# A seventh accumulator in the opening of an fp32 layer, its sums and transposes in one PSUM bank, and the modulation rows in runs of eight

## The chip, the cores and the metric

The kernel runs on one core of a Trainium2 chip. The metric is the device time of one execution, in microseconds (us). The shape is one sequence of 512 tokens with a model width of 1024, all in fp32.

## The reference

One layer: a feed-forward block, a mixer of mLSTM and attention with a forget gate, and a second feed-forward block. Each norm is modulated by rows that come from a small vector `c` by one product with `w_ada` (1024 x 9216).

```python
mod = jax.nn.silu(c) @ w_ada + b_ada
sh1, sc1, g1, sh2, sc2, g2, sh3, sc3, g3 = [m[:, None, :] for m in jnp.split(mod, N_MOD, axis=-1)]
u = rms_norm(x, ffn1_norm_g) * (1 + sc1) + sh1
x = x + 0.5 * g1 * swiglu(u, ffn1_w_in, ffn1_w_out)
...
def swiglu(u, w_in, w_out):
    a, b = jnp.split(u @ w_in, 2, axis=-1)
    return (jax.nn.silu(a) * b) @ w_out
```

The change lies in the first feed-forward block's `u @ w_in` (1024 x 5632: 22 column blocks of 128 for `a` and 22 for `b`) and in the rows of `mod` that are computed beside it.

## The kernel before, in words

Every fp32 product is made of three products of reduced-precision parts: `uh` and `ul` are the high part and the rest of the activations, `wh` and `wl` those of the weights. ACT makes a high part (L117), DVE the rest (L119). `mm3` (L142 to L144) issues hi x hi, hi x lo and lo x hi. In a slot 24 matmuls of 512 columns run behind one weight tile of 128 x 1024 (512 KB).

**The opening** is `start` (from L940). It loads `x`, computes the norm, and has 8 slices k of 128 of the model width. For each slice there are columns of `w_ada` (`ar`, four DMAs of 256 KB: shift v = 0 and scale v = 1, two halves each) and weights `raw` (block columns 0 to 2 of `a` and of `b`). Slice 0's shift and scale are summed over the 1024 rows by PE alone (`mod0`, 16 matmuls of 128 columns), slice 1's in part by PE (`mod1`) and otherwise by DVE; for slices 2 to 7, DVE makes products `ac` (`mod`, L1003) and PE adds up the partitions (`sums`, L1018). ACT turns the two sums into `m` (L1020, L1021), then `uh` and `uf` from the transposed x (L1026, L1028), and DVE `ul` (L1030). The transposes are `turn` (L977). A slice's gemm (L1084) is three passes over six accumulators, 3 blocks of `a` and 3 of `b`: `uh` with `wh`, `uh` with `wl`, `ul` with `wh`. The transposes of the next slice stand at the 7th matmul, its sums at the 12th. PE, ACT and DVE keep program order here (`pin`). All loads are issued by SP in program order; the weights use three buffers (`raw`), `wh` and `wl` four each.

**The slots** follow: `ffn_in` takes the other 19 blocks, first block 3 alone (two slots, one for `a` and one for `b`, `w_stat`), then 36 slots for pairs. Each calls `slot()`: `tick` runs what is due, `pw` brings one step of preparing the second weight matrix (loads `sa`, `sb`; stores `ws`), and `ada` one step of a modulation row (`ada_row`: 512 KB of `w_ada` in a `raw` buffer, one product on DVE, L323 or L325; eight steps make one row). The rows come in the order v = 3, 4, 2, 6; a slot with n % 6 = 5 has none. Behind the eighth step, `ada_sum` puts six steps into the coming ticks: 1 `fold` (ACT, L364, into a buffer of `wh`), 2 `high` (DVE L368, then ACT L369 into a buffer of `wl`), 3 `low` (DVE, L372), 4 `total` (PE, L377), 6 `bias`, 7 `put`.

PSUM has eight banks here: four from `gbank`, four from `tbank`. The accumulators take four and two, the column sums one (`cb`), the transposes one.

Of the kernel before, what the change touches and what calls it, by code (L numbers as in the profile page):

```python
# [47 lines left out]
class Layer:  # L48
# [261 lines left out]
    def ada_row(self, v, new, new_row, bank):  # L310
# [6 lines left out]
        for k in range(NK):  # L317
# [8 lines left out]
            if k == NK - 1:  # L326
                self.ada_sum(v, parts, new_row, bank)
# [26 lines left out]
    def ada_sum(self, v, parts, new_row, bank):  # L354
# [27 lines left out]
        for n, f in ((1, fold), (2, high), (3, low), (4, total), (6, bias), (7, put)):  # L382
            self.later(n, f)
# [24 lines left out]
    def ffn_in(self, w_in, j0, hp, tp, slot):  # L408

        if j0 % 2:  # L410
            ps = []
            for o in (0, FF):
                wt = self.w_stat(w_in, o + j0 * P)
                slot()
                ps.append(self.gbank())
                self.gemm_stat(ps[-1], wt, 0, T)
            self.pair_h(self.pair_s(ps[0], 0, T, tp), ps[1], j0, 0, T, hp, tp)
            self.lo_after = None
            j0 += 1
# [520 lines left out]
    def start(self, st, tp):  # L940
# [28 lines left out]
        def fill(n):  # L969

            for i in range(n):
                pin(nc.tensor.transpose(cb[:, 384:512], self.ident, self.ident))
# [5 lines left out]
        def ada_load(k):  # L978

            ars[k] = st.tile([P, NK, 2, P], F32, name=self.nm("ar"), tag="ar", bufs=7)  # L980
            halves = [(v, i) for v in range(2) for i in (0, 4)] if k == 0 else [(v, i) for i in (0, 4) for v in range(2)]
            for v, i in halves:
                nc.sync.dma_start(ars[k][:, i:i + 4, v, :], w_ada[i * P:(i + 4) * P, v * D + k * P:v * D + (k + 1) * P]
                                  .rearrange("(i p) n -> p i n", p=P))
        def mod0(v):

            for i in range(NK):
                pin(nc.tensor.matmul(cb[:, 128 * (v + 1):128 * (v + 2)], ars[0][:, i, v, :], self.ccol[:, i:i + 1].to_broadcast([P, P]),
# [15 lines left out]
        sh = [P, 2, NJ0 * P]  # L1004
        def load(k):
            raws[k] = self.raw(sh, [(lambda t, i=i: t[:, i, :],
                                     w_in[k * P:(k + 1) * P, i * FF:i * FF + NJ0 * P]) for i in range(2)])
# [5 lines left out]
        def w_lo(k):  # L1013
            hi, lo = ws[k]
            pin(nc.vector.tensor_tensor(lo, raws.pop(k), hi, op=SUB))
        def sums(k):
            for v in range(2):
                pin(nc.tensor.matmul(cb[:, 2 * k + v:2 * k + v + 1], accs[k][:, v, :], self.one, start=True, stop=True))  # L1018
        def affine(k, m, c, b):
            pin(nc.scalar.activation(m[:, 0:1], c[0], AF.Identity, bias=b[0]))  # L1020
            pin(nc.scalar.activation(m[:, 1:2], c[1], AF.Identity, scale=self.colC[:, 8 + k:9 + k], bias=b[1]))  # L1021
        def u_hi(k):
            m = sp.tile([P, 2], F32, name=self.nm("m"), tag="m", bufs=4)
            c = (cb[:, 2 * k:2 * k + 1], cb[:, 2 * k + 1:2 * k + 2]) if k else (cb[:, 128:129], cb[:, 256:257])
            affine(k, m, c, base if k == 1 else (self.colC[:, 16 + k:17 + k], self.colC[:, 24 + k:25 + k]))
# [5 lines left out]
        for k in range(3):  # L1031
# [6 lines left out]
        acc_ps = [self.gbank() for _ in range(4)] + [self.tbank() for _ in range(2)]  # L1038
        cb = self.tbank()
        fill(30)  # L1040
# [11 lines left out]
        mod0(0)  # L1052
        turn(0, (0, 1))
        turn(1, (0, 1))
        mod0(1)
        turn(0, (2, 3))
        mod1()
        w_hi(0)
        w_lo(0)
        u_hi(0)  # L1060
        mc, mb = [sp.tile([P, 2], F32, name=self.nm("m"), tag="m", bufs=4) for _ in range(2)]
# [10 lines left out]
        for k in range(NK):  # L1072
# [5 lines left out]
            for i, (p, b) in enumerate((p, b) for p in range(3) for b in range(2 * NJ0)):  # L1078
                if n < NK and i == 7:
# [834 lines left out]
```

## Time and profile before

| | us |
|---|---|
| median of 3 runs | 1303.6 |
| lowest, highest | 1303.08, 1305.67 |
| profiled execution | 1304.69 |
| its span | 1302.9 |
| PE busy in the span | 1288.7 (99%) |
| DVE, ACT busy | 982.1 (75%), 657.1 (50%) |

The profile is of one execution. Its span is the time from the first to the last recorded instruction. PE is TensorE's matmuls, PEld its weight loads, DVE VectorE, ACT ScalarE, SP SyncE, which issues most of the DMAs. The page gives PE's granted clock as 9 tenths or more in all 40 slices. A timeline row is one instruction or several of one kind in succession: its start, its length, and in brackets the idle time of the engine before it with what ended that. The length of a matmul (0.39 us for 512 columns) overlaps that of the next, so the step from start to start is what it costs.

### The profile page before, as it was taken

To read this page: it belongs to the slowest core of one execution; us is meant where nothing else is said; L and a number is where in the kernel's file an instruction comes from. 1 tells how busy PE (TensorE), PEld (TensorE's weight loads), DVE (VectorE), ACT (ScalarE), POOL (GpSimd) and SP (SyncE) were. 2 spreads that over 40 slices of the span, in tenths; PEclk is the share of its full clock that TensorE was granted. 3 is DMA by queue.
4 is the path that set the end of the run, shared out by engine and by line. 5 is a ranking of instruction groups with operands and counts; after the bars stand their busy time and mean duration, and the time that the engine had idled before them with its cause. 6 is when DMAs were issued, how large, how long until landed. Compare 5 with 4: busy or idle time off the path is not lost.

```text
span 1302.9 us, 17823 instructions
## 1 busy us (share of the span) xinstructions
PE 1288.7 (99%) x6241; PEld 1080.2 (83%) x6241; DVE 982.1 (75%) x1764; ACT 657.1 (50%) x1086; POOL 34.9 (3%) x73
## 2 busy tenths in 40 slices
PE   7999999999999999999999999999999999999998
PEld 6787888878889888888888888888898888888887
DVE  6877777778788868989897866778977656635787
ACT  5523223256567656666575786343683223223741
POOL 1000000000010011000000100000000000000000
PEclk9999999999999999999999999999999999999999
DMA  9988988765864634556455985776649867634574
GB/s 287 276 287 291 313 291 308 240 177 184 310 184 118 193 108 136 153 151 161 131 127 159 269 184 153 231 245 203 194 136 333 278 228 265 229 99 136 170 264 149
DMA packets 248330, 272.02 MB, mean 209 GB/s; under 512 B 57824, under 2 KB 185472, under 8 KB 248240
## 3 DMA queue, kind: packets, MB, share of 16 engines
q1 hardware_dynamic: 241104, 254.55, 63.3%
q10 hardware_dynamic: 4384, 7.88, 2.0%
q0 software_dynamic: 2752, 8.45, 1.9%
q8 instruction: 49, 0.80, 0.3%
q14 instruction: 41, 0.34, 0.1%
HBM read 227.77 MB, written 43.06 MB: 208 GB/s over the span
## 4 chain that ended last, share of the span: by engine, by line
PE 71%; DVE 4%; ACT 2%; issue 1%; DMA 1%; DVEq 0%; ACTq 0%; SPq 0%
PE g L144 18%; PE g L143 18%; PE g L142 18%; PE t L142 4%; PE t L143 4%; PE t L144 4%; PE t L1500 1%; PE t L1470 1%; PE t L1440 1%; PE t L1441 1%; ACT wh L117 0%; DVE wl L760 0%; DVE wl L119 0%; PE t L299 0%; DVE x L614 0%
## 5 line engine op out<-in xcount | busy, mean ns | idle before, releaser
L117 ACT ACTIVATE wh<-raw 128x1024 fp32r<-128x1024 f32 (+2 forms) x238 | 240.1, 1015 | 355.4 <-DMA raw<-in_ffn_w_in_dram 127.5
L119 DVE TENSOR_TENSOR wl<-raw,wh 128x1024 fp32r<-128x1024 f32 (+2 forms) x238 | 276.6, 1167 | 146.7 <-ACT wh L117 139.5
L144 PE MATMUL g<-uh,wl 128*128 128x512 f32 (+1 forms) x880 | 340.3, 387 | 1.6 <-DVE wl L119 1.6
L142 PE MATMUL g<-uh,wh 128*128 128x512 f32 (+1 forms) x880 | 341.0, 387 | 0.2 <-ACT wh L117 0.2
L143 PE MATMUL g<-ul,wh 128*128 128x512 f32 (+1 forms) x880 | 339.2, 385 | 0.0
L144 PEld LDWEIGHTS g<-uh,wl 128*128 128x128 f32 x880 | 165.3, 188 | 36.6 <-DVE wl L119 3.5
L142 PEld LDWEIGHTS g<-uh,wh 128*128 128x128 f32 x880 | 165.4, 188 | 33.3 <-issue 0.8
L143 PEld LDWEIGHTS g<-ul,wh 128*128 128x128 f32 x880 | 165.4, 188 | 32.6
L142 PE MATMUL g<-wh,uh 128*128 128x512 f32 (+1 forms) x256 | 97.6, 381 | 0.0
L144 PE MATMUL g<-wh,ul 128*128 128x512 f32 (+1 forms) x256 | 96.6, 377 | 0.0
L143 PE MATMUL g<-wl,uh 128*128 128x512 f32 (+1 forms) x256 | 96.5, 377 | 0.0
L325 DVE SCALAR_TENSOR_TENSOR acc<-raw,ccol,acc 128x1024 f32<-128x1024 f32 (+1 forms) x49 | 54.8, 1129 | 46.5 <-DMA raw<-in_w_ada_dram 46.3
L143 PE MATMUL t<-wl,A 128*128 128x512 f32 x176 | 68.6, 390 | 0.8 <-DVE wl L119 0.8
L142 PE MATMUL t<-wh,A 128*128 128x512 f32 x176 | 68.7, 390 | 0.0
L144 PEld LDWEIGHTS g<-wh,ul 128*128 128x128 f32 x256 | 48.2, 188 | 8.9
L143 PEld LDWEIGHTS g<-wl,uh 128*128 128x128 f32 x256 | 48.3, 188 | 8.4
L142 PEld LDWEIGHTS g<-wh,uh 128*128 128x128 f32 x256 | 48.2, 188 | 8.2
L142 PE MATMUL g<-yh,wh 128*128 128x512 f32 x128 | 49.9, 390 | 0.0
L144 PE MATMUL g<-yh,wl 128*128 128x512 f32 x128 | 49.8, 389 | 0.0
L143 PE MATMUL g<-yl,wh 128*128 128x512 f32 x128 | 49.8, 389 | 0.0
L1451 ACT ACTIVATE S<-S,mn 128x128 f32<-128x128 f32 (+1 forms) x64 | 35.6, 557 | 25.2 <-DVE mn L1443 15.8
L465 ACT ACTIVATE A<-E 128x768 fp32r<-128x768 f32 x22 | 18.6, 845 | 51.4 <-DVE E L464 51.0
(403 smaller groups left out, 2295.0 us busy)
## 6 DMA issues: line engine op xcount, KB each, us to landing
raw<-in_ffn_w_in_dram SPq DMA_DIRECT2D x80, 512.0 KB
raw<-in_w_ada_dram SPq DMA_DIRECT2D x48, 512.0 KB
raw<-in_w_mix_dram SPq DMA_DIRECT2D x46, 512.0 KB
sa<-in_ffn_w_out_dram SPq DMA_DIRECT2D x22, 512.0 KB
sb<-in_ffn_w_out_dram SPq DMA_DIRECT2D x44, 256.0 KB
ws<-sa SPq DMA_DIRECT2D x22, 512.0 KB
ws<-sb SPq DMA_DIRECT2D x44, 256.0 KB
raw<-ws SPq DMA_DIRECT2D x44, 256.0 KB
```

Source lines behind the costliest of these rows:

```text
L117: nc.scalar.activation(hi, src, AF.Copy)
L119: self.last_lo = nc.vector.tensor_tensor(lo, src, hi, op=SUB)
L142: pin(mm(ps, lh, rh, start=start, stop=False, skip_group_check=on))
L143: pin(mm(ps, lh, rl, start=False, stop=False, skip_group_check=on))
L144: self.last_mm = pin(mm(ps, ll, rh, start=False, stop=stop, skip_group_check=on))
L325: nc.vector.scalar_tensor_tensor(a, r[:, s], c, a, op0=MUL, op1=ADD)
L465: nc.scalar.activation(A1[:, 0:3, :], E[:, 0:3, :], AF.Copy)
L1440: nc.tensor.matmul(ps[:, :w], q[:, s], k[:, :w], start=True, stop=False)
L1441: nc.tensor.matmul(ps[:, :w], q[:, s], kl[:, :w], start=False, stop=True)
L1451: nc.scalar.activation(S[:, ws], S[:, ws], AF.Exp, scale=-1.0, bias=m, accum_out=sm[:, qb:qb + 1])
L1470: tr = lambda b, c, qb, kb: nc.tensor.transpose(b[:, c:c + P], S[:, P_OFF[qb] + kb * P:P_OFF[qb] + (kb + 1) * P], self.ident)
L1500: nc.tensor.matmul(po[:, q0:], vt[:, kb, i, :], Px[:, o:o + T - q0], start=n == 1, stop=n == 8)
```

## The change

1. The opening has seven accumulators: block 3 of `a` is the seventh. Its weights per slice are 448 KB in place of 384. `ffn_in` starts with block 3 of `b` alone, so there are 37 slots in place of 38; `s3` is the silu of the seventh accumulator.
2. `sums` takes its own `tbank`. Seven accumulators leave one bank to sums and transposes together, which now take turns in it; the sums of the next slice stand at the 10th matmul of a slice and the transposes at the 15th, of 21. `m` is computed right behind the sums. Slice 0's column sums (`mod0`) go into banks of accumulators.
3. The first weights (`load(0)`) are issued between the shift columns and the scale columns of slice 0. The fill transposes are 28 in place of 30.
4. The modulation rows skip slots 8, 9, 18, 19 and 28, so they come in runs of eight. The sum of v = 6 starts one tick later (`wait`).

```diff
--- before.py
+++ after.py
@@ -307,7 +307,7 @@
                      self.uh[k][:, c0:c1], self.ul[k][:, c0:c1], k == 0, k == NK - 1)
 
 
-    def ada_row(self, v, new, new_row, bank):
+    def ada_row(self, v, new, new_row, bank, wait=0):
 
 
         nc, A = self.nc, self.A
@@ -324,7 +324,7 @@
                 else:
                     nc.vector.scalar_tensor_tensor(a, r[:, s], c, a, op0=MUL, op1=ADD)
             if k == NK - 1:
-                self.ada_sum(v, parts, new_row, bank)
+                self.ada_sum(v, parts, new_row, bank, wait)
             yield
 
     def ada_early(self, v, yb, bank):
@@ -351,7 +351,7 @@
                 self.ada_sum(v, parts, lambda: yb[5][0:2, :], bank)
             yield
 
-    def ada_sum(self, v, parts, new_row, bank):
+    def ada_sum(self, v, parts, new_row, bank, wait=0):
         nc, A = self.nc, self.A
         g = {}
         rows = lambda a: a.rearrange("o (h n) -> (o h) n", h=2)
@@ -380,7 +380,7 @@
         def put():
             nc.sync.dma_start(rows(self.mod_d[v:v + 1, :]), g["br"])
         for n, f in ((1, fold), (2, high), (3, low), (4, total), (6, bias), (7, put)):
-            self.later(n, f)
+            self.later(n + wait, f)
 
     def mod_load(self, v):
         r = self.sp.tile([16, P], F32, name=self.nm("mr"), tag="mr", bufs=1)
@@ -405,16 +405,14 @@
         return t
 
 
-    def ffn_in(self, w_in, j0, hp, tp, slot):
+    def ffn_in(self, w_in, j0, hp, tp, slot, s=None):
 
         if j0 % 2:
-            ps = []
-            for o in (0, FF):
-                wt = self.w_stat(w_in, o + j0 * P)
-                slot()
-                ps.append(self.gbank())
-                self.gemm_stat(ps[-1], wt, 0, T)
-            self.pair_h(self.pair_s(ps[0], 0, T, tp), ps[1], j0, 0, T, hp, tp)
+            wt = self.w_stat(w_in, FF + j0 * P)
+            slot()
+            ps = self.gbank()
+            self.gemm_stat(ps, wt, 0, T)
+            self.pair_h(s, ps, j0, 0, T, hp, tp)
             self.lo_after = None
             j0 += 1
         for j in range(j0, NJ, 2):
@@ -969,23 +967,23 @@
         def fill(n):
 
             for i in range(n):
-                pin(nc.tensor.transpose(cb[:, 384:512], self.ident, self.ident))
+                pin(nc.tensor.transpose(fb[:, 0:P], self.ident, self.ident))
         def turn(k, tbs):
             if k not in bt:
                 bt[k] = self.tbank()
             for tb in tbs:
                 pin(nc.tensor.transpose(bt[k][:, tb * P:(tb + 1) * P], xn[tb, k // 4][:, k % 4 * P:(k % 4 + 1) * P], self.ident))
-        def ada_load(k):
-
-            ars[k] = st.tile([P, NK, 2, P], F32, name=self.nm("ar"), tag="ar", bufs=7)
-            halves = [(v, i) for v in range(2) for i in (0, 4)] if k == 0 else [(v, i) for i in (0, 4) for v in range(2)]
-            for v, i in halves:
+        def ada_load(k, vs=(0, 1)):
+
+            if k not in ars:
+                ars[k] = st.tile([P, NK, 2, P], F32, name=self.nm("ar"), tag="ar", bufs=7)
+            for v, i in [(v, i) for i in (0, 4) for v in vs]:
                 nc.sync.dma_start(ars[k][:, i:i + 4, v, :], w_ada[i * P:(i + 4) * P, v * D + k * P:v * D + (k + 1) * P]
                                   .rearrange("(i p) n -> p i n", p=P))
         def mod0(v):
 
             for i in range(NK):
-                pin(nc.tensor.matmul(cb[:, 128 * (v + 1):128 * (v + 2)], ars[0][:, i, v, :], self.ccol[:, i:i + 1].to_broadcast([P, P]),
+                pin(nc.tensor.matmul(acc_ps[4 + v][:, 0:P], ars[0][:, i, v, :], self.ccol[:, i:i + 1].to_broadcast([P, P]),
                                      start=i == 0, stop=i == NK - 1))
         def mod1():
 
@@ -1001,10 +999,10 @@
         def mod(k, i0, i1):
             for i in range(i0, i1):
                 pin(nc.vector.scalar_tensor_tensor(accs[k], ars[k][:, i], self.ccol[:, i:i + 1], accs[k], op0=MUL, op1=ADD))
-        sh = [P, 2, NJ0 * P]
+        sh, na = [P, (2 * NJ0 + 1) * P], (NJ0 + 1) * P
         def load(k):
-            raws[k] = self.raw(sh, [(lambda t, i=i: t[:, i, :],
-                                     w_in[k * P:(k + 1) * P, i * FF:i * FF + NJ0 * P]) for i in range(2)])
+            raws[k] = self.raw(sh, [(lambda t, i=i: t[:, i * na:na + i * NJ0 * P],
+                                     w_in[k * P:(k + 1) * P, i * FF:i * FF + (NJ0 + 1 - i) * P]) for i in range(2)])
         def w_hi(k):
             hi = self.wp.tile(sh, F32R, name=self.nm("wh"), tag="wh", bufs=4)
             lo = self.wp.tile(sh, F32R, name=self.nm("wl"), tag="wl", bufs=4)
@@ -1013,31 +1011,38 @@
         def w_lo(k):
             hi, lo = ws[k]
             pin(nc.vector.tensor_tensor(lo, raws.pop(k), hi, op=SUB))
+        def affine(k, m, c, b, vs=(0, 1)):
+            for v in vs:
+                pin(nc.scalar.activation(m[:, v:v + 1], c[v], AF.Identity, bias=b[v],
+                                         **({"scale": self.colC[:, 8 + k:9 + k]} if v else {})))
         def sums(k):
+            c = self.tbank()
             for v in range(2):
-                pin(nc.tensor.matmul(cb[:, 2 * k + v:2 * k + v + 1], accs[k][:, v, :], self.one, start=True, stop=True))
-        def affine(k, m, c, b):
-            pin(nc.scalar.activation(m[:, 0:1], c[0], AF.Identity, bias=b[0]))
-            pin(nc.scalar.activation(m[:, 1:2], c[1], AF.Identity, scale=self.colC[:, 8 + k:9 + k], bias=b[1]))
+                pin(nc.tensor.matmul(c[:, v:v + 1], accs[k][:, v, :], self.one, start=True, stop=True))
+            ms[k] = sp.tile([P, 2], F32, name=self.nm("m"), tag="m", bufs=6)
+            affine(k, ms[k], (c[:, 0:1], c[:, 1:2]), base if k == 1 else col(k))
         def u_hi(k):
-            m = sp.tile([P, 2], F32, name=self.nm("m"), tag="m", bufs=4)
-            c = (cb[:, 2 * k:2 * k + 1], cb[:, 2 * k + 1:2 * k + 2]) if k else (cb[:, 128:129], cb[:, 256:257])
-            affine(k, m, c, base if k == 1 else (self.colC[:, 16 + k:17 + k], self.colC[:, 24 + k:25 + k]))
+            m = ms[k]
             pin(nc.scalar.activation(self.uh[k], bt[k], AF.Identity, scale=m[:, 1:2], bias=m[:, 0:1]))
             ufs[k] = self.tmp(tp, "uf")
             self.last_uf = pin(nc.scalar.activation(ufs[k], bt[k], AF.Identity, scale=m[:, 1:2], bias=m[:, 0:1]))
         def u_lo(k):
             self.last_ul = pin(nc.vector.tensor_tensor(self.ul[k], ufs[k], self.uh[k], op=SUB))
-        for k in range(3):
+        ms = {}
+        col = lambda k: (self.colC[:, 16 + k:17 + k], self.colC[:, 24 + k:25 + k])
+        ada_load(0, (0,))
+        load(0)
+        ada_load(0, (1,))
+        for k in range(1, 3):
             ada_load(k)
             load(k)
         sq(0, 0)
         sq(0, 1)
         self.cols()
         self.u_tiles()
-        acc_ps = [self.gbank() for _ in range(4)] + [self.tbank() for _ in range(2)]
-        cb = self.tbank()
-        fill(30)
+        fb = self.tbank()
+        fill(28)
+        acc_ps = [self.gbank() for _ in range(4)] + [self.tbank() for _ in range(3)]
         for tb in (1, 2):
             sq(tb, 0)
             sq(tb, 1)
@@ -1049,16 +1054,18 @@
         rs.append(chain(1))
         norm(2, 0, True)
         norm(3, 0)
-        mod0(0)
-        turn(0, (0, 1))
-        turn(1, (0, 1))
-        mod0(1)
-        turn(0, (2, 3))
-        mod1()
         w_hi(0)
         w_lo(0)
+        ms[0], mc, mb = [sp.tile([P, 2], F32, name=self.nm("m"), tag="m", bufs=6) for _ in range(3)]
+        c0 = [acc_ps[4 + v][:, 0:1] for v in range(2)]
+        mod0(0)
+        affine(0, ms[0], c0, col(0), (0,))
+        turn(0, (0, 1))
+        turn(0, (2, 3))
+        mod0(1)
+        affine(0, ms[0], c0, col(0), (1,))
         u_hi(0)
-        mc, mb = [sp.tile([P, 2], F32, name=self.nm("m"), tag="m", bufs=4) for _ in range(2)]
+        mod1()
         base = mb[:, 0:1], mb[:, 1:2]
         w_hi(1)
         mod_first(1, True, 2)
@@ -1075,13 +1082,13 @@
                 ada_load(k + 3)
                 load(k + 3)
             wh, wl = ws[k]
-            for i, (p, b) in enumerate((p, b) for p in range(3) for b in range(2 * NJ0)):
-                if n < NK and i == 7:
-                    turn(n, range(NT) if k else (2, 3))
-                if n < NK and i == 12:
+            for i, (p, b) in enumerate((p, b) for p in range(3) for b in range(2 * NJ0 + 1)):
+                if n < NK and i == 10:
                     sums(n)
-                s = slice(b // 2 * P, (b // 2 + 1) * P)
-                pin(nc.tensor.matmul(acc_ps[b], (wl if p == 1 else wh)[:, b % 2, s], self.ul[k] if p == 2 else self.uh[k],
+                if n < NK and i == 15:
+                    turn(n, range(NT))
+                c = b % 2 * na + b // 2 * P
+                pin(nc.tensor.matmul(acc_ps[b], (wl if p == 1 else wh)[:, c:c + P], self.ul[k] if p == 2 else self.uh[k],
                                      start=k == 0 and p == 0, stop=k == NK - 1 and p == 2))
             if n < NK:
                 u_hi(n)
@@ -1600,19 +1607,20 @@
             with tc.tile_pool(name="f1h", bufs=1) as hp:
                 for j in range(NJ0):
                     self.pair_h(self.pair_s(acc_ps[2 * j], 0, T, tp), acc_ps[2 * j + 1], j, 0, T, hp, tp)
+                s3 = self.pair_s(acc_ps[2 * NJ0], 0, T, tp)
                 new = lambda: [tp.tile([P, D], F32, name=self.nm("acc"), tag="xn", bufs=1)]
                 row = lambda: tp.tile([2, 512], F32, name=self.nm("br"), tag="gb", bufs=2)
-                ada = (s for v in (3, 4, 2, 6) for s in self.ada_row(v, new, row, self.tbank if v < 6 else self.gbank))
+                ada = (s for v in (3, 4, 2, 6) for s in self.ada_row(v, new, row, self.tbank if v < 6 else self.gbank, v // 6))
                 pw = self.pair_weights(A["ffn1_w_out"][0], hp)
                 n = 0
                 def slot():
                     nonlocal n
                     self.tick()
                     next(pw, None)
-                    if n % 6 < 5:
+                    if n not in (8, 9, 18, 19, 28):
                         next(ada, None)
                     n += 1
-                self.ffn_in(A["ffn1_w_in"][0], NJ0, hp, tp, slot)
+                self.ffn_in(A["ffn1_w_in"][0], NJ0, hp, tp, slot, s3)
                 cols = {}
                 def load():
                     cols["r"] = self.mod_load(3)
```

On SP, the loads behind `x` in the opening (`ar_158`: columns of slice 0; `raw_163`, later `raw_161`: its weights; `ar_166`: columns of slice 1; `raw_171`: its weights), before:

```order
L983 DMA ar_158<-in_w_ada_dram 128x4x128 x4
L107 DMA raw_163<-in_ffn_w_in_dram 128x384 x2
L983 DMA ar_166<-in_w_ada_dram 128x4x128 x4
L107 DMA raw_171<-in_ffn_w_in_dram 128x384 x2
L983 DMA ar_174<-in_w_ada_dram 128x4x128 x4
L107 DMA raw_179<-in_ffn_w_in_dram 128x384 x2
```

and now:

```order
L981 DMA ar_158<-in_w_ada_dram 128x4x128 x2
L107 DMA raw_161<-in_ffn_w_in_dram 128x512
L107 DMA raw_161<-in_ffn_w_in_dram 128x384
L981 DMA ar_158<-in_w_ada_dram 128x4x128 x2
L981 DMA ar_166<-in_w_ada_dram 128x4x128 x4
L107 DMA raw_171<-in_ffn_w_in_dram 128x512
L107 DMA raw_171<-in_ffn_w_in_dram 128x384
L981 DMA ar_174<-in_w_ada_dram 128x4x128 x4
```

The weights of slice 0 moved ahead of two of the four loads of its columns, and each weight tile's first piece grew from 384 to 512 columns.

On PE, the second half of slice 0 (`g_`, `t_` accumulators; `t_305` the transposes of slice 1, `t_215` the sums), before:

```order
L1084 MATMUL t_214<-uh_193,wh_322 128x512
L1084 MATMUL g_209<-uh_193,wl_323 128x512
L977 MATMUL t_305<-ident,xn_290 128x128
L977 MATMUL t_305<-ident,xn_292 128x128
L1084 MATMUL g_210<-uh_193,wl_323 128x512
L1084 MATMUL g_211<-uh_193,wl_323 128x512
L1084 MATMUL g_212<-uh_193,wl_323 128x512
L1084 MATMUL t_213<-uh_193,wl_323 128x512
L1084 MATMUL t_214<-uh_193,wl_323 128x512
L1018 MATMUL t_215<-one,ac_337 128x1 x2
L1084 MATMUL g_209<-ul_201,wh_322 128x512
```

and now (`t_365` the sums, `t_376` the transposes, both in the one bank that the seven accumulators leave):

```order
L1091 MATMUL g_239<-uh_193,wl_294 128x512
L1091 MATMUL g_240<-uh_193,wl_294 128x512
L1021 MATMUL t_365<-one,ac_333 128x1 x2
L1091 MATMUL g_241<-uh_193,wl_294 128x512
L1091 MATMUL t_242<-uh_193,wl_294 128x512
L1091 MATMUL t_243<-uh_193,wl_294 128x512
L1091 MATMUL t_244<-uh_193,wl_294 128x512
L1091 MATMUL g_238<-ul_201,wh_293 128x512
L975 MATMUL t_376<-ident,xn_271 128x128
L975 MATMUL t_376<-ident,xn_273 128x128
L975 MATMUL t_376<-ident,xn_289 128x128
L975 MATMUL t_376<-ident,xn_291 128x128
```

The sums moved from the 12th to the 10th matmul and ahead of the transposes; between the two stand five matmuls, behind the transposes six.

On ACT, behind the slots, where the second product of the block starts (`wh_` splits of weights, `fo_` the fold of v = 6, `hl_` its high part, `A_` operands), before:

```order
L117 ACTIVATE wh_2384<-raw_445_2382 128x512
L364 ACTIVATE fo_2390<-acc_1973 64x1024
L117 ACTIVATE wh_2415<-raw_2412 128x1024
L117 ACTIVATE wh_2421<-raw_454_2419 128x512
L369 ACTIVATE hl_2425<-acc_1973 64x1024
L117 ACTIVATE wh_2455<-raw_2452 128x1024
```

and now:

```order
L117 ACTIVATE wh_2383<-raw_449_2381 128x512
L117 ACTIVATE wh_2410<-raw_2407 128x1024
L117 ACTIVATE wh_2416<-raw_456_2414 128x512
L364 ACTIVATE fo_2422<-acc_2055 64x1024
L489 ACTIVATE A_461_2442<-Ra_758 128x512
L489 ACTIVATE A_461_2442<-Rb_759 128x512
L117 ACTIVATE wh_2451<-raw_2448 128x1024
L117 ACTIVATE wh_2457<-raw_466_2455 128x512
L117 ACTIVATE wh_2492<-raw_2489 128x1024
L369 ACTIVATE hl_2461<-acc_2055 64x1024
```

The fold moved behind two splits, and its high part behind three more.

## Rows read from the trace of the kernel before

**Rows 1.** The page, busy time of each engine: us, share of the span, instructions.
```profile
PE 1288.7 (99%) x6241; PEld 1080.2 (83%) x6241; DVE 982.1 (75%) x1764; ACT 657.1 (50%) x1086; POOL 34.9 (3%) x73
```

**Rows 2.** Waits of PE, whole span: line, waited for, us in total, times, longest.
```profile
PE g L144 <- DVE wl L119: 1.6, 2, 1.4
...
PE t L143 <- DVE wl L119: 0.8, 1, 0.8
```

**Rows 3.** Timeline of PE, opening: start, us, engine line op, [idle before <-releaser].
```profile
13.49 1.95 PE L988 MATMUL t<-ccol,ar 128*128 128x128 f32 x16
...
16.54 0.61 PE L994 MATMUL t<-ccol,ar 128*128 128x1 f32 x4 [0.28 <-DMA ar<-in_w_ada_dram]
...
17.00 1.19 PE L1084 MATMUL g<-uh,wh 128*128 128x512 f32 x4
...
20.51 0.61 PE L1018 MATMUL t<-one,ac 128*128 128x1 f32 x4 [0.25 <-DVE ac L1003]
...
22.58 1.19 PE L1084 MATMUL g<-uh,wh 128*128 128x512 f32 x4
...
24.31 0.60 PE L977 MATMUL t<-ident,xn 128*128 128x128 f32 x4
24.66 0.94 PE L1084 MATMUL g<-uh,wl 128*128 128x512 f32 x3
...
27.00 0.61 PE L1018 MATMUL t<-one,ac 128*128 128x1 f32 x4 [0.94 <-DVE ac L1003]
...
29.02 1.20 PE L1084 MATMUL g<-uh,wh 128*128 128x512 f32 x4
...
37.59 0.50 PE L1018 MATMUL t<-one,ac 128*128 128x1 f32 x4
...
55.20 1.20 PE L1084 MATMUL g<-uh,wh 128*128 128x512 f32 x4
...
59.45 0.47 PE L142 MATMUL g<-uh,wh 128*128 128x512 f32 x1
```

**Rows 4.** Timeline of DVE, opening.
```profile
14.71 0.56 DVE L1012 CAST wh<-raw 128x768 fp32r<-128x768 f32 x1 [1.54 <-DMA raw<-in_ffn_w_in_dram]
...
24.43 1.00 DVE L1003 SCALAR_TENSOR_TENSOR ac<-ar,ccol,ac 128x256 f32<-128x256 f32 x2 [1.28 <-DMA ar<-in_w_ada_dram]
```

**Rows 5.** Waits of all engines from 0 to 300 us.
```profile
PEld g L1084 <- ACT uh L1026: 2.5, 7, 0.4
```

**Rows 6.** Timeline of ACT, slice 4's sums and its uh.
```profile
38.13 0.26 ACT L1020 ACTIVATE m<-t,colC 128x1 f32<-128x1 f32 x1 [1.59 <-PE t L1018]
...
38.67 0.78 ACT L1026 ACTIVATE uh<-t,m 128x512 fp32r<-128x512 f32 x1
```

**Rows 7.** Timelines of ACT and PE, slot 11 at 120 us.
```profile
116.96 1.06 ACT L117 ACTIVATE wh<-raw 128x1024 fp32r<-128x1024 f32 x1 [4.09 <-DMA raw<-in_ffn_w_in_dram]
...
120.14 0.39 PE L143 MATMUL g<-ul,wh 128*128 128x512 f32 x1
...
121.87 0.50 PE L144 MATMUL g<-uh,wl 128*128 128x512 f32 x1 [1.35 <-DVE wl L119]
```

**Rows 8.** Timelines of DVE and PE, weights' last step and first use, slots 4 and 8.
```profile
79.82 1.23 DVE L119 TENSOR_TENSOR wl<-raw,wh 128x1024 fp32r<-128x1024 f32 x1 [1.21 <-ACT wh L117]
...
82.01 0.39 PE L144 MATMUL g<-uh,wl 128*128 128x512 f32 x1
...
102.56 1.22 DVE L119 TENSOR_TENSOR wl<-raw,wh 128x1024 fp32r<-128x1024 f32 x1
...
103.83 0.50 PE L144 MATMUL g<-uh,wl 128*128 128x512 f32 x1
```

**Rows 9.** Timelines of ACT and PE, the stall at 274 us.
```profile
273.18 1.58 ACT L117 ACTIVATE wh<-raw 128x1024 fp32r<-128x1024 f32 x2 [1.28 <-DVE acc L368]
...
274.30 0.50 PE L142 MATMUL t<-wh,A 128*128 128x512 f32 x1
...
275.56 0.50 PE L143 MATMUL t<-wl,A 128*128 128x512 f32 x1 [0.76 <-DVE wl L119]
```

## The prediction

> **What bounds the kernel now.** I read the page first: PE is busy 1288.7 of 1302.9 us [rows 1], and the change keeps the matmul work (24 matmuls of 512 columns go from the slots into the opening), so only what PE waits for can move. The wait list of PE [rows 2] names what is left: 1.6 us for `wl` at L144 and 0.8 us at L143, both from DVE. The opening has waits of its own in its timeline. So I read three stretches: the opening, slot 11 at 120 us, and 274 us, and in each the engine that ends last ahead of PE's step. Between its slots PE steps 0.227 us per 512-column matmul: (103.83 - 82.01) / 96, four slots of 24 [rows 8].
>
> **The opening, before.** The first gemm starts at 17.00 behind 4 column matmuls at 16.54, which waited for DMA `ar` [rows 3]. The loads come in one stream: the first weights land at 14.71 (DVE's cast waits for them [rows 4]), and the first half of `ar` slice 1, two transfers of 256 KB, at 16.54: 1.83 us for 512 KB. Then come slices of three passes, with starts at 17.00, 22.58, 29.02 and, after five more, 55.20 [rows 3]; a steady slice takes (55.20 - 29.02) / 5 = 5.24 us, the last, without sums and transposes, 59.45 - 55.20 = 4.25 us, so 0.231 to 0.236 per matmul. Slices 0 and 1 wait for DVE's products of the sums: 0.25 us at 20.51, 0.94 us at 27.00 [rows 3], the latter because DVE itself waited 1.28 us for `ar` [rows 4]. Each slice start waits for `uh`: 2.5 us of weight-load waits in 7 [rows 5]. What of these 0.36 us each reaches PE's matmuls lies between 0 and 0.36; I take 0.07, near the lower end, since PE's own wait list has no such row near its top [rows 2].
>
> **The change, part by part.**
>
> *First weights ahead of the scale's columns, 448 KB of them in place of 384.* The 64 KB cost 64 / 512 x 1.83 = 0.23 us in the stream. `ar` slice 1's half lands at 16.54 + 0.23 = 16.77; its 4 matmuls take 17.00 - 16.54 = 0.46 us, so the gemm can start at 17.23. The other chain: the scale's columns land 0.23 later than the weights did, at 14.94; half of PE's eight scale matmuls wait for that, 1.0 of the 1.95 us that 16 take [rows 3], to 15.95; then ACT's `m` and `uh` (0.54 and 0.78 [rows 6]) end at 17.2 to 17.3. First gemm **+0.25 us**.
>
> *Slice 0.* DVE's chain to the sums hangs on `ar` and shifts by less than its 0.23: from 20.51 to some 20.6. PE, which comes to the sums after 10 matmuls (12 before), is there at 17.25 + 10 x 0.231 = 19.6 and waits 1.0 us, 0.25 before. From the sums' start to the next slice it took 22.58 - 20.51 = 2.07 us with 6 matmuls; now 5 more (1.16) and the transposes (24.31 to 24.66, 0.35 [rows 3]): slice 1 at 24.15. Before it was 22.58, and the three matmuls of the seventh accumulator (0.69) are paid back in the slots: 24.15 - 23.27 = **+0.88**, cumulated.
>
> *Slice 1.* DVE waits for `ar` slice 2, which now has 128 KB more ahead of it: 24.43 + 0.46 = 24.89 [rows 4]; from there the sums are 27.00 - 24.43 = 2.57 us away, as before: 27.45. Slice 2 starts 2.02 + 1.16 + 0.35 later, at 31.0, against 29.02 + 1.38: cumulated **+0.6**. The load comes less late than PE has more work, so the delay shrinks.
>
> *Slices 2 to 7.* The transposes now stand 6 matmuls before the end of a slice. The sums come at the 10th matmul, so ACT's `m` is done before them, and only `uh` follows: 0.78 and what passes between PE and ACT (0.54, 37.59 to 38.13 [rows 3, 6]), 1.3 us, against 6 x 0.231 = 1.4 us. The 0.07 us at six slice starts goes: **-0.4**. Opening in all **+0.2 us**. Bounds: +1.2 if DVE's chain is late in slices 2 and 3 too (the 0.6 not won back, and 0.25 twice), -0.9 if the 0.94 us of slice 1 is covered by the longer slice.
>
> *Sums and transposes in one bank.* The transposes must wait until ACT has read the sums. In the trace the sums start at 37.59 and `m` is done when `uh` starts, 38.67 [rows 3, 6]: 1.08 us. The transposes come 1.6 us after the sums' start (5 matmuls, 1.16, and the sums themselves, 0.46 by the four at 16.54). So the wait is hidden with 0.5 us to spare: **0**. Below 0 it can't come; above, it costs what ACT is late. The Trainium skill, PSUM — Partial Sum Buffer, section "Summary: rules for kernel authors", speaks against the sharing: who reads PSUM while matmuls run should take another bank, and guard with semaphores by bank; by it PE's next write would stand behind ACT's read in each of seven slices. That is rival D.
>
> *Fill 28 for 30, the first columns' sums in accumulator banks, more `m` buffers.* All lie ahead of the first gemm, which hangs on `ar`: 0, and if that load came earlier the chain over `m` and `uh` would bind at the same time.
>
> *Slots 8 and 9 without a row (120 us).* Slot 11's first L144 came at 121.87 where 120.14 + 0.23 was due: 1.50 us, and it lasts 0.50 in place of 0.39, 0.11 more. ACT got its weights only at 116.96, after 4.09 us of waiting for DMA, and DVE, which makes `wl`, was the last to come [rows 7]: v = 3's fold, high and low stood in slots 9 to 11, where v = 4's first rows took raw buffers and DVE. Now v = 3 ends in slot 7 and its fold and high fall into slots 8 and 9, which have no row: DVE loses two products there and the stream 2 x 512 KB. **-1.6**; bounds 0 and -1.6.
>
> *Runs of eight.* Rows on end drain the lead of the weights, the first use by PE less the end of `wl`: in slot 4, the fifth row of five, 82.01 - 81.05 = 0.96 us; in slot 8, in spite of a slot without a row between, 103.83 - 103.78 = 0.05 [rows 8]. Slots 5 to 7 now have rows behind slot 4's 0.96 (some 0.6 more, as the opening's last slice is 0.6 longer). The row at slot 8 names no wait even at 0.05 (it lasts 0.50 us in place of 0.39), so I take **+0.2**; bounds 0 and a stall like that of slot 11, 1.6.
>
> *v = 6's sum one tick later (274 us).* PE waited 275.56 - 274.30 - 0.23 = 1.03 us at L143, and the two matmuls of 0.50 us there cost 0.1 each. ACT's splits began at 273.18 after 1.28 us of waiting for DVE's high add [rows 9]: the fold's tile has one of the four buffers of `wh`, and ACT's order has the fold ahead of both splits. Now both splits stand ahead of the fold. **-1.2**; bounds 0 (the next splits wait in their place) and -1.2.
>
> *One slot fewer.* 24 x 0.227 us leave the slots, 24 x 0.231 enter the opening: 0 (+0.1).
>
> **Sum**: 0.2 - 1.6 + 0.2 - 1.2 = -2.4. The profiled execution took 1304.69 (span 1302.9); it would take 1302.3. The median of the runs, 1303.6, lies 1.1 lower, so I set **1301.2**. A measurement of this kernel tells about 0.2% (2.6 us) from no change.
>
> **Rivals.**
> A, the forecast: 1301.2, own range 1300.2 to 1302.2; of its 0.40, 0.18 lies beyond -0.2%.
> B, the opening gains too: PE's 0.69 us more per slice give DVE and the stream time, so slice 1's wait shrinks: -0.9 in place of +0.2, **1300.1**. For: the 1.28 us of DVE is the only load that is late by much [rows 4]. Against: 128 KB more stand ahead of it. Chance 0.24.
> C, one of the two stalls moves instead of going (the fold's `wh` buffer is missed at the next splits, or slots 5 to 7 run dry): 1.2 back, **1302.4**. For: slot 8's lead of 0.05 [rows 8]. Chance 0.20.
> D, the shared bank puts ACT on PE's path: in seven slices the transposes wait for `m`. It decides from the point where ACT reaches the sums over 0.5 us late. Behind two ACT instructions of 0.78, `m` ends 1.08 + 1.56 = 2.6 us after the sums' start, the transposes come 1.0 late, 7 x 1.0 = 7.0: 1308.2, **slower**. For: ACT works in order, and `uf`, the split and the next first product stand ahead of `m`. Against: at 38.13 ACT had waited 1.59 us for the sums [rows 6]. Chance 0.10.
> E, neither stall goes and the opening is even: **1303.8**, no difference. For: DVE's and the stream's total over the slots stay the same. Chance 0.06.
>
> **How the numbers follow.** Faster by over 0.2%: 0.18 of A and 0.22 of B, 0.40. Slower: D, 0.10. The rest 0.50. The range takes in A, C, E and most of B, and leaves out D: 1299.2 to 1303.8.
>
> **What would show it.** First gemm at 17.2, slice 1 at 24.1, slice 2 at 31.0, then 5.85 us per slice without a wait for `uh`; no wait of the transposes for ACT; no PE step over 0.35 us in slots 8 to 12, none over 0.4 between 265 and 285 us; steps up to 0.4 in slots 5 to 7. PE's wait list loses its rows of L144 and L143. The prediction is wrong if the transposes wait for ACT slice after slice, if `wl` stands in the wait list with over 1 us at another place of the slots, or if slices 2 to 7 take more than 5.95 us each.

## The result: slower, and where the time went

The changed kernel takes 1310.0 us in the median of 6 runs (1307.85 to 1312.37), the kernel before 1303.87 in as many: a ratio of 1.0044, interval 1.0032 to 1.0056. The forecast was 1301.2, the range ended at 1303.8. The profiled execution has a span of 1307.1 us (1308.83 as a whole) against 1302.9.

The page after, busy time of each engine:

```profile
PE 1292.7 (99%) x6239; PEld 1081.1 (83%) x6239; DVE 982.8 (75%) x1763; ACT 656.1 (50%) x1085; POOL 34.1 (3%) x73
```

PE is busy 4.0 us longer than in [rows 1], with the same matmuls but for two fill transposes. This is not waiting: the time is inside the matmuls. The list of PE's waits after, behind the 5.6 us for the first load of all:

```profile
PE g L144 <- DVE wl L119: 2.2, 2, 2.0
PE t L1021 <- ACT wh L1010: 0.8, 1, 0.8
```

The two waits of [rows 2] are gone from their places; one of 2.0 us has come elsewhere. The row of L1021 is the wait before the first sums, at 20.81 below. In the built program these sums wait for DVE's products, and of ACT only for `uf`, which ended at 17.98; DVE's last product ended at 20.66. So they waited for DVE, as forecast, and not for the `wh` that the profile names. The timeline of PE in the opening, after (columns as in rows 3):

```profile
16.70 0.61 PE L992 MATMUL t<-ccol,ar 128*128 128x1 f32 x4 [0.26 <-DMA ar<-in_w_ada_dram]
17.36 1.21 PE L1091 MATMUL g<-uh,wh 128*128 128x512 f32 x4
...
20.81 0.58 PE L1021 MATMUL t<-one,ac 128*128 128x1 f32 x4 [0.84 <-ACT wh L1010]
...
24.33 1.07 PE L1091 MATMUL g<-uh,wh 128*128 128x512 f32 x4
...
26.61 0.50 PE L1021 MATMUL t<-one,ac 128*128 128x1 f32 x4
...
30.04 1.07 PE L1091 MATMUL g<-uh,wh 128*128 128x512 f32 x4
...
38.16 0.50 PE L1021 MATMUL t<-one,ac 128*128 128x1 f32 x4
...
39.52 0.39 PE L1091 MATMUL g<-ul,wh 128*128 128x512 f32 x1
39.75 0.60 PE L975 MATMUL t<-ident,xn 128*128 128x128 f32 x4
...
58.66 1.07 PE L1091 MATMUL g<-uh,wh 128*128 128x512 f32 x4
...
63.45 0.47 PE L142 MATMUL g<-uh,wh 128*128 128x512 f32 x1
```

The opening is better than forecast. It ends at 63.45 with one slot of 5.44 us fewer to come: 63.45 - 5.44 - 59.45 = -1.4 us. The sums of slice 2 wait for nothing (26.61; 0.94 us at 27.00 in [rows 3]). The slot at 120 us [rows 7] has no stall now; the stall at 274 us [rows 9] is down to one step of 0.59 us near 270. A new one stands in slot 33, below.

What outweighs all this is a smooth loss. The table by stretch of PE, first the kernel before, then the changed one (stretch in us, length, busy us and count of instructions, granted clock, DMA share, GB/s):

```profile
180.00:220.00 40.00, 40.00 (x178) 1.00 0.92 321
300.00:340.00 40.00, 39.94 (x176) 1.00 0.59 201
830.00:870.00 40.00, 40.00 (x178) 1.00 0.83 251
1205.00:1245.00 40.00, 40.00 (x177) 1.00 0.52 161
```

```profile
180.00:220.00 40.00, 40.00 (x178) 1.00 0.94 319
300.00:340.00 40.00, 39.94 (x171) 1.00 0.65 214
830.00:870.00 40.00, 40.00 (x176) 1.00 0.83 245
1205.00:1245.00 40.00, 40.00 (x172) 1.00 0.54 164
```

In the slots, 180 to 220 us, PE gets through the same 178 instructions. In the second products of both feed-forward blocks it gets through 171 and 172 in place of 176 and 177, at a granted clock of 1.00, without a gap. A step there is 0.233 us in place of 0.227 (means from start to start, the changed kernel and the one before: 0.2331 and 0.2269 over 290 to 372 us, 0.2331 and 0.2267 over 1204 to 1290); in the branch product around 850 us it is 0.229. Followed matmul by matmul, the changed trace loses 2.3 us against that of before between 289 and 372 us, 1.3 between 790 and 940 and 2.3 between 1204 and 1290: 5.9 us.

What these stretches share: one operand of their matmuls lies in a tile that is allocated behind the small tile `m` (`A`, `Ra`, `Rb`, `mr`, `yh`, `yl`), the other in one that lies ahead (`wh`, `wl`). In the slots both lie ahead (`uh`, `wh`). In the second products the tile behind `m` is the stationary operand (128 columns) and `wh` or `wl` the moving one (512); in the branch product `yh` and `yl` move. (My expectations of e2 and e5 call `A`, `Ra`, `Rb` and `mr` moving operands; they are stationary ones.) Six buffers of `m` in place of four, of 32 bytes each, move all that follows by 64 bytes: the built program has `A` at byte 137120 before and 137184 now, `wh` at 79264 in both. Before, the distance is 57856, a multiple of 256, and so it is for `uh`, `yh` and the second block's `A`.

The changed trace holds a control of its own. Between 911 and 939 us products with `mo`, which lies ahead of `m`, alternate with products with `mr`, which lies behind it, amid the same traffic. The groups of PE there (count, busy us, mean ns of one matmul):

```profile
L142 PE MATMUL t<-wh,mo 128*128 128x512 f32 x24 | 9.3, 390 | 0.0
...
L142 PE MATMUL t<-wh,mr 128*128 128x512 f32 x8 | 3.2, 396 | 0.0
```

From start to start that is 0.227 us with `mo` and 0.233 with `mr`; in the kernel before both take 0.227.

### The profile page after: what moved, and what is told of

It is laid out like the page before. It is cut to its first block, busy times and chain, and to the rows that moved or that the text cites. A ratio compares the mean times of both kernels' runs of the same rounds, so it can differ in the third digit from the quotient of the medians.

```text
span 1307.1 us, 17822 instructions
## 1 busy us (share of the span) xinstructions
PE 1292.7 (99%) x6239; PEld 1081.1 (83%) x6239; DVE 982.8 (75%) x1763; ACT 656.1 (50%) x1085; POOL 34.1 (3%) x73
## 4 chain that ended last, share of the span: by engine, by line
PE 76%; DMA 10%; DVE 8%; ACT 3%; issue 1%; SPq 1%; ACTq 0%; DVEq 0%
PE g L144 18%; PE g L143 18%; PE g L142 18%; DMA raw<-in_ffn_w_in_dram 5%; PE t L142 4%; PE t L144 4%; PE t L143 4%; DMA raw<-in_w_ada_dram 3%; DVE wl L119 2%; PE g L1091 1%; ACT wh L117 1%; PE t L1507 1%; DVE acc L325 1%; PE t L1477 1%; DMA raw<-ws 1%
```

## The experiments

**Theory 1**: a 512-column matmul is slower where the places of its two operands in SBUF differ by 32 or 64 bytes from a multiple of 256, and the 64 bytes of `m` make the loss. **Rival**: the changed order of loads and rows makes these stretches slower through traffic. **Theory 2**, on the slots: the new stall comes from DVE's order, not from late weights.

### e1: the changed kernel with four buffers of m

```diff
-tag="m", bufs=6
+tag="m", bufs=4
```

> The changed kernel with four buffers of the small tile m, as before, in place of six: every tile allocated behind m goes back by 64 bytes to its place in the kernel before, and no instruction changes its order. Theory 1 (place of tiles): the matmuls of the two second feed-forward products (moving operands A, Ra, Rb) go back from 0.2333 to 0.2267 us a step, and the same at the branch product; some 5.9 us go, about 1303 to 1304 by runs, and a span near 1301. Rival (the changed order of loads and rows makes these stages slower, by traffic): the step stays at 0.233 and the time at 1309 to 1310.

1304.26 us (10 runs), ratio to before 1.0003, interval 0.9990 to 1.0015; span 1302.6, where I had expected one near 1301. By stretch:

```profile
300.00:340.00 40.00, 39.84 (x173) 1.00 0.66 215
830.00:870.00 40.00, 40.00 (x178) 1.00 0.82 258
1205.00:1245.00 40.00, 40.00 (x177) 1.00 0.53 158
```

The branch product and the second block are back at the counts of before (the first stretch has 173 because some waits are longer there, 1.1 us above the step in all where the kernel before has 0.6; its mean step is 0.227). 5.7 us are gone with two numbers changed that have no part in the work. What is left of the change is no difference.

### e2, e3, e4: the kernel before with six, five and three buffers of m

```diff
-tag="m", bufs=4
+tag="m", bufs=6
```

> The kernel before with six buffers of the small tile m in place of four: the only difference is that everything behind m lies 64 bytes further on. Theory 1: the step of the matmuls with A, Ra, Rb and mr as moving operand goes from 0.2267 to 0.2333 us and the time up by 5 to 6.5 us, to 1309 to 1310, with opening and slots as before. Rival (traffic, order): no change, 1303 to 1305.

> The kernel before with five buffers of m: a shift of 32 bytes. It asks whether any shift costs, or only some places. If what counts is the place within 64 bytes, 32 is another class than 0 and 64, and the step would be unlike both. If only 64 is bad (place within 128 or 256 bytes), the time stays at 1303 to 1305. If each 32 bytes add, about half of the 5.9 us: 1306 to 1307.

> The kernel before with three buffers of m: a shift of 32 bytes the other way. A place within 64 bytes as the rule: the same time as the shift of 32 bytes forward. A place within 128 bytes: not the same by need. The three buffers may add a short wait in the opening, up to 0.5 us.

e2 (64 bytes on): 1310.68 us, ratio 1.0055 (1.0036 to 1.0074). e3 (32 on): 1312.4, 1.0070 (1.0055 to 1.0085). e4 (32 back): 1311.18, 1.0063 (1.0048 to 1.0078). By stretch, e2 and then e3:

```profile
180.00:220.00 40.00, 40.00 (x177) 1.00 0.93 325
300.00:340.00 40.00, 39.93 (x170) 1.00 0.59 192
830.00:870.00 40.00, 40.00 (x177) 1.00 0.78 239
1205.00:1245.00 40.00, 40.00 (x172) 1.00 0.53 160
```

```profile
300.00:340.00 40.00, 40.00 (x173) 1.00 0.60 201
830.00:870.00 40.00, 40.00 (x173) 1.00 0.79 233
1205.00:1245.00 40.00, 40.00 (x173) 1.00 0.56 169
```

The kernel before becomes as slow as the changed one by nothing but the place of its tiles, so the rival falls. Each of the three shifts costs, one way and the other; e4 has the counts 178, 171, 173 and 173. I had offered e3 half the loss or none; it has all of it. In the traces of e3 and e4, at 32 bytes, the branch product is also at 0.233 (173), at 64 only at 0.229 (177); between the times of the three runs this makes no difference beyond their intervals.

### e5: everything shifted

```diff
         self.cp = pool("const", bufs=1)
+        self.cp.tile([P, 16], F32, name="pad")
```

> The kernel before with 64 bytes in front of the first pool, so that every tile of the kernel, stationary and moving, lies 64 bytes further on (the last tiles as in the changed kernel). Theory 1a (what counts is the place of the moving tile against that of the stationary tile): all steps stay at 0.2267 us, span near 1302 to 1303. Theory 1b (what counts is the moving tile's own place): all large stages, the slots with uh among them, go to 0.233: 5300 matmuls of 512 columns by 0.006, some 25 to 30 us more.

One run: 1304.4 us, span 1302.6. By stretch:

```profile
180.00:220.00 40.00, 40.00 (x178) 1.00 0.93 321
300.00:340.00 40.00, 40.00 (x176) 1.00 0.62 208
830.00:870.00 40.00, 40.00 (x178) 1.00 0.83 253
1205.00:1245.00 40.00, 40.00 (x177) 1.00 0.50 157
```

`A` is here where e2 has it, and the step is that of before. So it isn't the tile's own place that counts but its place against others. That the other is the matmul's second operand, and not a tile that some other engine uses, e5 can't tell, since it keeps all distances; the rows of `mo` and `mr` do, which differ amid the same traffic. Theory 1a stands.

### e6, e7: the opening alone, the rows alone

Both with four buffers of `m`. In e6 the rows skip a slot in six again and v = 6's sum has its old tick; in e7 the opening is that of before.

```diff
e6, against the change:
-                    if n not in (8, 9, 18, 19, 28):
+                    if n % 6 < 5 or n == 35:
e7, against the kernel before:
-                    if n % 6 < 5:
+                    if n not in (8, 9, 18, 19, 28):
```

> Seven accumulators, shared bank and first weights as in the change, with the rows skipping a slot in six as before (5, 11, 17, 23, 29), no later sum for v = 6, and m with four buffers, so that all other tiles keep their places. Theory (the opening gains 1.4 us, as the changed kernel's first slot at 63.45 against 59.45 + 5.44 shows): slots from 63.5, the stalls of 1.5 us near 120 and 1.1 near 272 to 274 still there; span 1301 to 1302, runs 1302. Rival (the extra weights delay the first rows in the slots): stalls of 1 us more in the slots, no gain.

> The kernel before with the rows skipping slots 8, 9, 18, 19 and 28 and the sum of v = 6 a tick later; opening as before. Theory: stalls at 120 and 274 us go (2.7 us), and a stall of 1.5 to 2.5 us comes in slots 32 to 34, where v = 6's rows run behind v = 2's with one slot between and v = 2's sum is among them; net 0 to -1. Rival (that stall comes from the seven-accumulator opening): no stall there, -2.5 us.

e6: 1305.93 us, ratio 1.0018 (1.0004 to 1.0032). The slots begin at 63.55, so the opening has its gain, but it is given back. Its stalls of [rows 7] and [rows 9] are both there:

```profile
125.06 0.50 PE L144 MATMUL g<-uh,wl 128*128 128x512 f32 x1 [0.92 <-DVE wl L119]
...
275.81 0.50 PE L143 MATMUL t<-wl,A 128*128 128x512 f32 x1 [0.77 <-DVE wl L119]
```

Beside them stand steps of 0.54 at 131 us, 0.47 and 0.51 at 181 and 192, and 0.77 and 0.73 at 270, which the kernel before doesn't have. The rival of this run was right on the time: no gain. It had put the added stalls at the first rows, though; they stand at 131 to 270 us, and why they come isn't shown.

e7: 1301.38 us, ratio 0.9977 (0.9966 to 0.9988), and no PE wait at all in the list for 57 to 290 us. Both stalls are gone, and the stall of slot 33 doesn't come, so that one needs the seven-accumulator opening, whose slots carry other blocks at the same numbers. Here too the rival was nearer than the theory that I had written down.

### e8: the free slot moved

```diff
-                    if n not in (8, 9, 18, 19, 28):
+                    if n not in (8, 9, 18, 28, 29):
```

> The changed kernel with m of four buffers and the rows skipping slots 8, 9, 18, 28 and 29 in place of 8, 9, 18, 19 and 28: the second free slot goes from between v = 4 and v = 2 to between v = 2 and v = 6, where the leads of the weights had fallen to 0.05 us. Theory: the stall of 1.7 to 2.1 us near 246 us shrinks under 0.5 us, new ones near 170 to 200 stay under 0.5: span near 1300.5, runs 1301.5 to 1302.5, faster than both by 1 to 2 us. Rival (the stall only moves into run three): same time as with the change's gaps.

1307.24 us, ratio 1.0021 (1.0011 to 1.0030): a miss. PE waits 4.4 us for `wl` in four places (and 1.9 for `wh` and `Ra`), and DVE's timeline shows why for the longest of them:

```profile
230.59 1.28 DVE L325 SCALAR_TENSOR_TENSOR acc<-raw,ccol,acc 128x1024 f32<-128x1024 f32 x1 [5.77 <-DMA raw<-in_w_ada_dram]
231.79 1.22 DVE L119 TENSOR_TENSOR wl<-raw,wh 128x1024 fp32r<-128x1024 f32 x1
```

DVE stands idle for 5.77 us before a row's product whose load is late, with the `wl` that PE waits for behind it in its queue. So moving the free slot did not help, and DVE's order is what to test. The changed kernel's slot 33, PE, ACT and DVE:

```profile
244.82 0.39 PE L143 MATMUL g<-ul,wh 128*128 128x512 f32 x1
247.17 0.50 PE L144 MATMUL g<-uh,wl 128*128 128x512 f32 x1 [1.96 <-DVE wl L119]
...
239.41 1.06 ACT L117 ACTIVATE wh<-raw 128x1024 fp32r<-128x1024 f32 x1 [3.35 <-PE g L144]
...
239.24 1.28 DVE L325 SCALAR_TENSOR_TENSOR acc<-raw,ccol,acc 128x1024 f32<-128x1024 f32 x1
244.69 1.28 DVE L325 SCALAR_TENSOR_TENSOR acc<-raw,ccol,acc 128x1024 f32<-128x1024 f32 x1 [4.18 <-DMA raw<-in_w_ada_dram]
245.90 1.22 DVE L119 TENSOR_TENSOR wl<-raw,wh 128x1024 fp32r<-128x1024 f32 x1
```

ACT has the high part done at 240.47. DVE could make `wl` then; its order has a second row product first, which waits 4.18 us for its load.

### e9, e10: the products tied behind the weights

```diff
                 else:
-                    nc.vector.scalar_tensor_tensor(a, r[:, s], c, a, op0=MUL, op1=ADD)
+                    with self.tc.issue_after(self.last_lo.ins):
+                        nc.vector.scalar_tensor_tensor(a, r[:, s], c, a, op0=MUL, op1=ADD)
```

> The changed kernel with m of four buffers, and each row's products on DVE (from the second on) tied behind the last weight split, so that no two products of a row stand ahead of a wl on DVE. Theory: the stall near 246 us comes from DVE's order, where two products, the second waiting 4.2 us for its 512 KB of w_ada, stand ahead of a wl whose weights are there; it goes (under 0.4 us), others stay small; span 1300 to 1301, 1 to 2 us under the changed kernel with m of four buffers. Rival (the loads themselves are late for the weights too): the stall stays at 1.5 to 2 us.

> The kernel before with the new gaps and the later sum, and the same tie. There the slots have no stall over 0.35 us, so the tie can win nothing: 1301 to 1302, as with the rows alone. Slower by over 1 us would say that the tie costs where it isn't needed.

e9, on the changed kernel with four buffers of `m`: 1301.55 us, ratio 0.9982 (0.9973 to 0.9992), 2.7 under e1 (1.9 by the spans of the two traces). No step of PE over 0.36 us is left between 64 and 268 us. DVE at the same place:

```profile
242.85 1.23 DVE L119 TENSOR_TENSOR wl<-raw,wh 128x1024 fp32r<-128x1024 f32 x1 [2.12 <-ACT wh L117]
244.00 1.28 DVE L326 SCALAR_TENSOR_TENSOR acc<-raw,ccol,acc 128x1024 f32<-128x1024 f32 x1
245.85 1.23 DVE L119 TENSOR_TENSOR wl<-raw,wh 128x1024 fp32r<-128x1024 f32 x1 [0.57 <-ACT wh L117]
249.11 1.29 DVE L326 SCALAR_TENSOR_TENSOR acc<-raw,ccol,acc 128x1024 f32<-128x1024 f32 x1 [2.04 <-DMA raw<-in_w_ada_dram]
```

The product still waits for its load (2.04 us; 4.18 without the tie), but nothing that PE needs stands behind it. The tie moved loads too: ACT starts the high part of this slot's weights at 241.76 here and at 239.41 in the changed kernel. They are later, and still PE has no stall, so late weights were not its cause. Theory 2 holds.

e10, on the rows alone: 1300.34 us, ratio 0.9977 (0.9967 to 0.9986), the lowest median of all, though its interval can't be told from e7's. Both beat the kernel before and the changed one.

### e11, e12: two parts by themselves

```diff
e11, against e7:
-self.gbank, v // 6))
+self.gbank))
e12, against e1:
         ada_load(0, (0,))
-        load(0)
         ada_load(0, (1,))
+        load(0)
```

> The kernel before with the new gaps alone: the sum of v = 6 at its old tick. Theory (each of the two parts removes its own stall): the stall near 120 us is gone and a stall of 1.0 to 1.3 us stands near 272 us. Rival (the gaps already move the last row, so its sum falls elsewhere): no stall over 0.5 us near 265 to 280.

> The changed kernel with m of four buffers, its first weights behind all four loads of slice 0's columns as before. Theory (the first weights are what the first gemm waits for least): first gemm at 17.2 to 17.4 as with the weights ahead, slots from 63.4 to 63.6, so that part of the change is worth 0. Rival (the weights ahead win DVE 0.5 us or more, which makes the first split late otherwise): first gemm at 17.8 or later.

e11, one run: 1304.52 us, span 1302.7. The stall near 120 is gone, that near 272 is there, and larger than expected. PE's timeline, then its table by stretch:

```profile
271.20 0.39 PE L142 MATMUL t<-wh,A 128*128 128x512 f32 x1
273.89 0.80 PE L143 MATMUL t<-wl,A 128*128 128x512 f32 x1 [2.30 <-DVE wl L119]
```

```profile
271.20:273.90 2.70, 0.40 (x3) 0.95 0.33 84
273.90:277.00 3.10, 3.10 (x7) 0.50 0.76 243
277.00:282.00 5.00, 5.00 (x23) 0.99 0.70 209
```

So each of the two parts removes its own stall, and the later sum is needed once the gaps have moved the last rows. e12, one run: first gemm at 17.44, slots from 63.73, against 17.31 and 63.51 in e1: between these two traces the first weights' place in the queue is worth some 0.2 us.

## Why the prediction was wrong, point by point

**The step that failed** is "Fill 28 for 30, the first columns' sums in accumulator banks, more `m` buffers: 0". I costed the buffers by the work they take part in and not by the tiles that they push along. They cost 5.9 us by the changed trace, 5.7 by e1, and 7.2 (4.7 to 9.6, by the ratio) when put into the kernel before (e2). No rival of mine was of this kind; the slower side that I offered, the shared bank, is not what happened.

**Shared bank, 0.** Right. In the steady slice the transposes follow the matmul ahead of them at its own step, 39.52 to 39.75, and PE waits for ACT's `m` in no slice. ACT has read the sums of 38.16 by 39.20, inside the 1.6 us of matmuls between:

```profile
38.69 0.51 ACT L1016 ACTIVATE m<-t,colC 128x1 f32<-128x1 f32 x2 [1.25 <-PE t L1021]
```

The Trainium skill, PSUM — Partial Sum Buffer, section "Summary: rules for kernel authors", asks for another bank where PSUM is read while matmuls run; the wait that I drew from it for rival D shows in no run. Rival D is out; that the time came near its 1308.2 is chance.

**Opening, +0.2; measured -1.4**, beyond its bound of -0.9. First gemm +0.25: 17.36 - 17.00 = +0.36. Slice 1 at 24.15: 24.33. Slice 2 at 31.0: 30.04. The step that failed there is the load of `ar` slice 2, which I had put at 24.89 by adding 128 KB. The products of slice 2 run through without a wait:

```profile
22.13 2.57 DVE L1001 SCALAR_TENSOR_TENSOR ac<-ar,ccol,ac 128x256 f32<-128x256 f32 x5
```

Why the load was there in time with more bytes ahead of it I haven't settled. Steady slices take (58.66 - 30.04) / 5 = 5.72 us where I had 5.85: the visible part of the `uh` wait was some 0.2 us and not 0.07, well within its bounds of 0 and 0.36. At a steady slice's start PE's steps were 0.31 and 0.34 us in the kernel before; now they are 0.23. So rival B had the right mechanism, but what it won was given back in the slots (e1, e6).

**Slots 8 and 9, -1.6.** Right: no step over 0.35 us from 64 to 244 us. **v = 6's sum, -1.2.** Half right: steps of 0.59 and 0.35 remain near 270, so some -0.75; e11 shows that without it the place costs more.

**Runs of eight, +0.2; measured +2.2** (247.17 - 244.82 - 0.23, and 0.11), beyond the bound of 1.6, in the fourth run and not in the first. The measure I used, the lead of the weights, was the wrong one: weights and their high part were there, and DVE's queue was held by a row. It is one of the signs of being wrong that I had named: `wl` in the wait list with over 1 us at another place of the slots. Rival C said that a stall would come elsewhere, by a drained lead or a held buffer; it came by a third way, the order on DVE.

**Together**: -1.4 - 1.6 + 2.2 - 0.75 = -1.5 for the parts that I had costed, +5.9 for the one that I had at nothing: +4.4, and the spans differ by 4.2. That this fits so closely is part luck. Followed matmul by matmul, the changed trace is 2.0 us ahead at 296 us, some 0.6 more than these parts give (small steps that only the kernel before has), and in the rest of the trace it loses some 0.5 us that the 5.9 do not count.

## What to carry to other kernels

After a change, count a steady stretch of matmuls in equal windows of both traces: fewer at the same clock and without gaps means that the matmul itself takes longer. The place of its operands is then a suspect that one run with the old places tests, as e1 did; here padding the pools so that the two operands of the big products lie a multiple of 256 bytes apart is what keeps the shorter step. Work that may wait for a late load should stand behind the work that another engine waits for, on the same queue; a free slot moved elsewhere (e8) did not replace that order here. And take a change apart before it is judged: here one part wins 0.23%, another nothing, and a buffer count hides both.

## What the runs showed of the hardware that I had not expected

A 512-column matmul of the second products takes 0.227 us a step when its operands' places differ by a multiple of 256 bytes, and 0.233 when the difference is 32 or 64 bytes off. The branch product takes 0.233 at 32 bytes too, but at 64 its three parts differ: 0.226 for `yh` with `wh`, 0.232 for `yh` with `wl`, 0.229 for `yl` with `wh`. So the distance is not the whole condition. Nor is a multiple of 256 always 0.227: the opening of the kernel before has 0.231 at such distances. Products of 256 columns of which one operand is shifted (`uh` with `fh` and `fl`) lose nothing: 0.115 to 0.119 us in e2 to e4, 0.120 before. The spacing of 128 bytes was not tried, nor which of the two reads is held up.

After the step of 2.69 us in e11 (PE idle for 2.30) the granted clock is 0.50 for the next 3.1 us, the lower of its two levels, with steps of 0.43 us, and then 0.99. After the stall of the kernel before [rows 7] (1.35 idle) and that of the changed one at 247.17 (1.96 idle) it stays at 1.00: the step behind is 0.34 and the ones after it 0.23 to 0.24.
